# Strassen's products for both down-projections of a two-FFN decoder layer, with their activation sums made in the up-projection

## The chip, the cores and the metric

The kernel runs on one core of a Trainium2 chip. The time is device microseconds from start to end of one execution; three runs of the kernel before are shown, and one more execution was taken apart by the hardware profiler.

## What is computed

One layer of a hybrid decoder on 1024 prompt tokens and 32 sample tokens (1056 columns together): half a SwiGLU feed-forward block, token mixing (windowed attention beside a diagonal state-space scan), and a second half feed-forward block. All is float32. The change concerns the last product of the two feed-forward blocks, with D_MODEL = 1024 and D_FF = 2816:

```
def swiglu(x, w1, w3, w2):
    return (jax.nn.silu(x @ w1) * (x @ w3)) @ w2

def trunk_layer(x, pos0, k_buf, v_buf, s_re, s_im, p):
    x = x + 0.5 * swiglu(rms_norm(x, p['ffn1_norm']), p['ffn1_w1'], p['ffn1_w3'], p['ffn1_w2'])
    h = rms_norm(x, p['mix_norm'])
    ...
    x = x + merged @ p['w_out']
    x = x + 0.5 * swiglu(rms_norm(x, p['ffn2_norm']), p['ffn2_w1'], p['ffn2_w3'], p['ffn2_w2'])
```

## The kernel before

Activations lie with features on the 128 partitions and the 1056 tokens as columns. For precision each float32 operand is kept as two parts, a rounded high part (a cast on ScalarE) and the remainder (a subtraction on VectorE), and each product of 128x128 weights with a column group is three matmuls, high x high, high x remainder, remainder x high (`passes`, L225 to L229).

The program goes through these stages: first up-projection, first down-projection, the projections `pj` of the token mixing, scan and attention, w_out, second up-projection, second down-projection.

**Up-projection** (`up`, L385). D_FF is 22 blocks of 128 rows. Block by block, w1 and w3 are multiplied at once with Strassen's seven products over two halves of the model dimension and two halves of the tokens (H = 528 columns, each as two pieces J = 264). `wprep` makes the weight sums, `combos` made the sums of activations once for all blocks. Of the first two blocks the products are made in the plain way (`plain`). The results of product number 4, 3, 1, 2, 5, 7, 6, in this order, are put together by VectorE into a tile `e`, and the block is stored to `hid` in HBM, half by half (L411, L417). In the first up-projection a `hook` works in the parameters of the state-space scan (`params`, `params_b`) beside the blocks, on GpSimd, with some transposes on TensorE.

**Down-projection** (`down`, L421). Plain: the 22 blocks of `hid` are read back in groups of 4, 4, 4, 4, 4, 2 (`GROUPS`), each cut into high part `hh` and remainder `hl`; for each of the 8 output blocks and 3 column groups of 352 a PSUM bank collects a group's products, and VectorE adds half of it to the residual `x` (L445). In the first down-projection the last group's results also feed the next norm (`run_last`, `xg_part`): on ScalarE the scaled high part `xh` and a square, on VectorE the remainder `xl`, on GpSimd the sum of squares.

A scheduler sets the order of the instructions on each engine and of the loads in SP's single list, save where `in_order` (L139) pins TensorE, VectorE and ScalarE to the order of the code. Tiles come from pools: 34 large ones of 1056 columns (`T`), 4 for raw weights (`wr`, 4 KB a partition), 8 each for high parts and remainders of weights (`wh`, `wl`), 5 small ones (`sq`), and eight PSUM banks.

Lines of a helper stand for many calls: L229 is every such matmul, L81 every addition, subtraction or product of two tiles on VectorE or GpSimd, L93 every fused multiply-add on VectorE, L102 every activation, L208 and L334 casts of weights, L430 the cast of `hid`.

## Time and profile before

| | |
|---|---|
| median of three runs | 2161.9 us (2157.95 to 2163.28) |
| the profiled execution | 2159.04 us |
| its span in the trace | 2157.3 us |
| TensorE busy | 2095.9 us, 97% |
| VectorE busy | 1385.5 us, 64% |
| ScalarE busy | 749.2 us, 35% |
| GpSimd busy | 375.2 us, 17% |
| DMA | 234.4 MB, mean 109 GB/s |

In the profile PE is TensorE's matmuls, PEld its weight loads, DVE VectorE, ACT ScalarE, POOL GpSimd, SP the engine that issues the loads and stores. A group of instructions is named by the tile it writes and those it reads. An arrow (<-) behind idle time names what ended the wait.

### The profile page before, as it was taken

The page shows a single profiled execution, that of the slowest core. Times are in us where ns is not written, and L with a number is a line of the kernel's source. Part 1 is how long each engine was busy: PE and PEld are TensorE (multiplying, and loading weights), DVE is VectorE, ACT ScalarE, POOL GpSimd, SP SyncE. Part 2 cuts the span into 40 slices and gives each one's busy share as a digit, 9 for nine tenths or more (in the row PEclk, how much of TensorE's full clock was granted, in tenths as well). Part 3 has the DMA queues.
Part 4 walks back from the last instruction along what each step waited for, and adds up shares of the span by engine and source line. Part 5 has one row for each costly group of instructions (what it writes and reads, how often), then busy time and mean ns, then how long its engine had stood idle before and what let it go on. Part 6 is the DMA issues. An engine that isn't in the chain of part 4 may idle for free.

```text
span 2157.3 us, 38133 instructions
## 1 busy us (share of the span) xinstructions
PE 2095.9 (97%) x15058; PEld 2065.8 (96%) x15058; DVE 1385.5 (64%) x2485; ACT 749.2 (35%) x1464; POOL 375.2 (17%) x759
## 2 busy tenths in 40 slices
PE   8899999999999999999899899998999999999999
PEld 7899999988999999999899899988999999999999
DVE  5886666665554375757877857688666666565433
ACT  4432444344321152235555733343222232332110
POOL 0017777673000041324100200000000000000000
PEclk9899999999999999999999999999999999999999
DMA  4122322335631135632222373321222221363212
GB/s 164 36 88 73 115 95 86 122 103 169 227 117 55 60 120 184 213 108 62 80 88 82 144 247 125 124 88 45 78 90 67 82 89 62 100 238 124 81 35 81
DMA packets 133075, 234.40 MB, mean 109 GB/s; under 512 B 26064, under 2 KB 62736, under 8 KB 132880
## 3 DMA queue, kind: packets, MB, share of 16 engines
q1 hardware_dynamic: 132896, 231.97, 32.4%
q8 instruction: 118, 1.93, 0.4%
q14 instruction: 61, 0.50, 0.1%
HBM read 164.98 MB, written 64.06 MB: 106 GB/s over the span
## 4 chain that ended last, share of the span: by engine, by line
PE 87%; DVE 8%; ACT 2%; issue 2%; DMA 2%; SPq 0%; DVEq 0%; ACTq 0%
PE P L229 36%; PE p L229 26%; PE pj L229 13%; PE pm L229 4%; PE Q L229 2%; DVE wl L81 1%; PE pg L229 1%; PE ss L684 1%; DVE B L93 1%; DVE Xl L81 1%; PE po L1111 1%; PE sc L1072 1%; DVE e L81 1%; DVE B L81 0%; PE pt L1096 0%
## 5 line engine op out<-in xcount | busy, mean ns | idle before, releaser
L229 PE MATMUL P<-Xh,wh 128*128 128x264 f32 x2240 | 642.6, 287 | 21.4 <-DVE e L81 14.3
L229 PE MATMUL P<-Xl,wh 128*128 128x264 f32 x2240 | 641.0, 286 | 0.0
L229 PE MATMUL P<-Xh,wl 128*128 128x264 f32 x2240 | 639.4, 285 | 0.0
L229 PEld LDWEIGHTS P<-Xh,wh 128*128 128x128 f32 x2240 | 425.5, 190 | 26.6 <-DVE e L81 9.4
L229 PEld LDWEIGHTS P<-Xl,wh 128*128 128x128 f32 x2240 | 425.2, 190 | 1.5 <-issue 1.5
L229 PEld LDWEIGHTS P<-Xh,wl 128*128 128x128 f32 x2240 | 425.0, 190 | 0.0
L229 PE MATMUL p<-hh,wh 128*128 128x352 f32 x1056 | 341.6, 324 | 5.6 <-DVE x L93 2.8
L229 PE MATMUL p<-hh,wl 128*128 128x352 f32 x1056 | 341.5, 323 | 0.0
L229 PE MATMUL p<-hl,wh 128*128 128x352 f32 x1056 | 341.0, 323 | 0.0
L81 DVE TENSOR_TENSOR wl<-wr,wh 128x512 fp32r<-128x512 f32 (+1 forms) x360 | 249.4, 696 | 99.8 <-ACT wh L334 73.8
L93 DVE SCALAR_TENSOR_TENSOR x<-p,x 128x352 f32<-128x352 f32 x288 | 149.9, 523 | 238.2 <-PE p L229 235.7
L208 ACT CAST wh<-wr 128x512 fp32r<-128x512 f32 (+1 forms) x200 | 119.3, 601 | 429.9 <-PE p L229 309.0
L81 DVE TENSOR_TENSOR e<-e,P 128x528 f32<-128x528 f32 (+1 forms) x250 | 169.4, 680 | 136.3 <-PE P L229 116.8
L229 PE MATMUL pj<-xh,wh 128*128 128x352 f32 x624 | 205.2, 329 | 6.7 <-DVE gt L81 5.6
L229 PEld LDWEIGHTS p<-hh,wh 128*128 128x128 f32 x1056 | 198.5, 188 | 6.9 <-DVE x L93 3.4
L229 PE MATMUL pj<-xl,wh 128*128 128x352 f32 x624 | 203.6, 326 | 0.0
L229 PE MATMUL pj<-xh,wl 128*128 128x352 f32 x624 | 203.4, 326 | 0.0
L229 PEld LDWEIGHTS p<-hl,wh 128*128 128x128 f32 x1056 | 199.3, 189 | 0.0
L229 PEld LDWEIGHTS p<-hh,wl 128*128 128x128 f32 x1056 | 198.7, 188 | 0.0
L334 ACT CAST wh<-wr 128x512 fp32r<-128x512 f32 x160 | 98.9, 621 | 266.5 <-PE P L229 233.2
L334 ACT CAST wh<-ws 128x512 fp32r<-128x512 f32 x120 | 74.6, 622 | 228.3 <-PE P L229 220.5
L229 PEld LDWEIGHTS pj<-xh,wh 128*128 128x128 f32 x624 | 118.5, 190 | 8.2 <-DVE gt L81 6.1
(601 smaller groups left out, 3469.6 us busy)
## 6 DMA issues: line engine op xcount, KB each, us to landing
hr<-hid SPq DMA_DIRECT2D x44, 528.0 KB
hid<-e SPq DMA_DIRECT2D x78, 264.0 KB
wr<-in_w_in SPq DMA_DIRECT2D x26, 512.0 KB
wr<-in_w3a SPq DMA_DIRECT2D x40, 256.0 KB
wr<-in_w1a SPq DMA_DIRECT2D x40, 256.0 KB
wr<-in_w2a SPq DMA_DIRECT2D x40, 256.0 KB
wr<-in_w3b SPq DMA_DIRECT2D x40, 256.0 KB
wr<-in_w1b SPq DMA_DIRECT2D x40, 256.0 KB
```

The source lines that it names most:

```text
L81: e.tensor_tensor(out=o, in0=a, in1=b, op=op)
L93: V.scalar_tensor_tensor(out=o, in0=a, scalar=s, in1=b, op0=op0, op1=op1)
L208: S.copy(h[:, 0:m, :], r[:, i:i + m, :])
L229: mark["pe"] = PE.matmul(ps, a, b, start=first and i == 0, stop=last and i == 2, **kw).ins
L334: S.copy(h, s)
L684: PE.matmul(ps, f32(ones), s[:, kk, :], start=a + i + kk == 0, stop=a == 1 and i + kk == 2)
L1072: PE.matmul(o, st[e_][:, q0:q0 + 128], kk[:, k0:k0 + nk * 128], start=i == 0, stop=False)
L1111: PE.matmul(po[:, 0:256], Vs[blk // 4][:, blk % 4, m // 2, :], P[:, a_, kb * 256:kb * 256 + 256], start=i == 0, stop=i == 2 * nk - 1)
```

## The change

Both down-projections are made with Strassen's seven products too. Here the inner dimension is split by block number: blocks 2k and 2k+1 are a pair, 11 pairs (`NK`). The outputs split into two halves of 512 rows, the tokens into two halves of 528. One product at a time goes over four output blocks, each with a whole PSUM tile of two banks, and over the 11 pairs in three steps of 3, 4 and 4 pairs (`GROUPS`). `DOPS` gives the order of the products and the quarters of the result to which each is added with its sign; products 7 and 6 go on in the PSUM tiles of 4 and 3.

The seven combinations of activations are made in the up-projection: products 2 and 5 need a quarter as it is, the other five a sum or difference of two half blocks (`hsums`, on VectorE, through a small `sq` tile), and all are stored in seven arrays `hc` in place of `hid`. Only the two plain blocks still go through `hid` and are read back. `operands` reads one array two pairs at a time, casts and subtracts as before, reads one or two quarters of w2, adds them (`WCOMB`), casts and subtracts. While the matmuls of one step run, `down` draws the operands of the next, two pieces per output block, and the results of the output block before; the first step's operands are made in the last block of the up-projection. The next norm's parts (`xg_half`) follow in the middle step of the product after the one that finishes a quarter. The whole down-projection stands under `in_order`. The parameter work of the hook moves by one block, w2 is packed by quarters on the host.

```diff
-GROUPS = 4, 4, 4, 4, 4, 2
+NK = NFF // 2
+GROUPS = 3, 4, 4
+DOPS = (4, ((2, 1),)), (7, ((0, 1),)), (2, ((2, 1), (3, -1))), (1, ((0, 1), (3, 1))), (5, ((1, 1), (0, -1))), (3, ((1, 1),)), (6, ((3, 1),))
...
+        def hsums(k, e0, e1, do):
...
+            for op in do:
+                f_, a, b = {6: lambda: (add, half(e0, 0), half(e0, 1)), 4: lambda: (sub, half(e1, 0), half(e0, 0)),
+                            7: lambda: (add, half(e1, 0), half(e1, 1)), 3: lambda: (sub, half(e0, 1), half(e1, 1)),
+                            1: lambda: (add, half(e0, 0), half(e1, 1))}[op]()
+                t = SQ("hs", w=H)
+                f_(t, a, b)
+                mark["hid"] = dma(hc[op][:, k, :], t).ins
...
+                if f == NFF - 1:
+                    ks = first_operands(w2)
...
-                        dma(hid[f, :, 0:H].rearrange("p (j c) -> p j c", j=2)[:, js, :], q)
+                        if odd:
+                            hsums(k, e0, e, (4,))
+                        else:
+                            dma(hc[2][:, k, :].rearrange("p (j c) -> p j c", j=2)[:, js, :], q)
...
-                        mark["hid"] = dma(hid[f, :, H:T], e[:, H:T]).ins
+                        if odd:
+                            dma(hc[5][:, k, :], e[:, H:T])
+                            hsums(k, e0, e, (7, 3, 1))
+                        else:
+                            hsums(k, e, None, (6,))
+                if f == f0 + 1:
+                    es_ = [TT("e") for _ in range(2)]
+                    for i in range(2):
+                        dma(es_[i], hid[i])
...
+                    hsums(0, *es_, (6, 4, 7, 3, 1))
...
+        def operands(w, op, k0, n, ks):
+
+            for k1 in range(k0, k0 + n, 2):
+                m = min(2, k0 + n - k1)
...
+                dma(raw, hc[op][:, k1:k1 + m, :])
+                S.copy(h, raw)
+                p, q, f_ = WCOMB[op]
+                s = [wr_p.tile([128, 8, 128], F32, tag="wr", name="wr")[:, 0:4 * m, :] for i in (p, q) if i is not None]
+                for t, i in zip(s, (p, q)):
+                    dma(t.rearrange("p (k m) c -> p k (m c)", k=m), w[i % 2, i // 2, :, k1:k1 + m])
+                if q is not None:
+                    f_(s[0], s[0], s[1])
+                    yield
+                unit, low = w_cast(s[0], 4 * m)
+                sub(l, raw, f32(h))
+                yield
+                for a in low:
+                    sub(*a)
+                    yield
+                ks += [(unit[i], (h[:, i, :], l[:, i, :])) for i in range(m)]
...
+            for i, (op, outs, g) in enumerate(steps):
...
+                for m, p in enumerate(P):
+                    for k, (wu, (h, l)) in enumerate(ks, k0):
+                        for j in range(2):
+                            js = slice(j * J, j * J + J)
+                            passes(p[:, j, 0:J], [t[:, m, :] for t in wu], (h[:, js], l[:, js]), opens and k == 0, k == NK - 1,
+                                   skip_group_check=not opens)
+                    while evac:
+                        evac.pop(0)()
+                    for _ in range(2):
+                        next(it, None)
+                    if extra and g == 1:
+                        extra.pop(0)()
+                    if ends:
+                        evac.append(partial(evacuate, x, op, outs, m, p, done, extra, i + 1 == len(steps)))
...
+        WCOMB = {1: (0, 3, add), 5: (0, 1, add), 2: (2, 3, add), 7: (1, 3, sub), 6: (2, 0, sub), 3: (0, None, None), 4: (3, None, None)}
...
-                if f > 5 and f % 2:
+                if f > 4 and f % 2 == 0:
...
-        hid = dr.tile([NFF, 128, T], F32, name="hid")
+        hid = dr.tile([2, 128, T], F32, name="hid")
+        hc = {op: dr.tile([128, NK, H], F32, name=f"hc{op}") for op in OPS}
...
+        with in_order():
+            down(I["w2a"], I["x"], x, ks, (1, 2, 0, 3), xg_half)
...
+        with in_order():
+            down(I["w2b"], xd2, x, ks, (3, 1, 2, 0), lambda b, m: dma(O["y"][m, :, b * H:b * H + H], x[m][:, b * H:b * H + H]))
```

How this moves the instructions, at three places. Numbers behind a name tell one buffer's use from another's. First VectorE's list in the middle of the first down-projection: before, with the additions to `x` behind every output block and column group (`p2` is the PSUM tile).

```order
L81 TENSOR_TENSOR wl_7139<-wr_7136,wh_7138 128x512
L93 SCALAR_TENSOR_TENSOR x5_6693<-p2_6962,x5_6693 128x352
L81 TENSOR_TENSOR hl_7103<-hr_7100,hh_7102 128x1056
L93 SCALAR_TENSOR_TENSOR x5_6693<-p2_6976,x5_6693 128x352
L93 SCALAR_TENSOR_TENSOR x5_6693<-p2_6990,x5_6693 128x352
```

And now, in the middle step of product 1: the weight sum, the activation remainder, the norm's pieces, the weight remainders.

```order
L84 TENSOR_TENSOR wr_8124<-wr_8124,wr_8125 128x1024
L84 TENSOR_TENSOR hl_8121<-hr_8119,hh_8120 128x1056
L96 SCALAR_TENSOR_TENSOR xl_8137<-x4_6835,vec_84,xh_8136 128x528
L84 TENSOR_TENSOR wl_8130<-wr_8124,wh_8129 128x512
L84 TENSOR_TENSOR wl_8133<-wr_8124,wh_8132 128x512
L96 SCALAR_TENSOR_TENSOR xl_8169<-x5_6836,vec_84,xh_8168 128x528
L84 TENSOR_TENSOR sq_8172<-sq_8172,sq_8140 128x528
L84 TENSOR_TENSOR wr_8204<-wr_8204,wr_8205 128x1024
L84 TENSOR_TENSOR hl_8201<-hr_8199,hh_8200 128x1056
```

Before, a group's preparation lay between additions, and the sum of squares was GpSimd's; now the sums of weights and of squares have come to this list, and the additions stand at a product's end only.

Second SP's list in the same stretch, before: one quarter of a megabyte of weights at a time, activations up to two groups ahead.

```order
L198 DMA wr_7538<-in_w2a 128x512
L428 DMA hr_7514<-hid_133 128x1056
L428 DMA hr_7904<-hid_133 128x1056
L198 DMA wr_7544<-in_w2a 128x512
L428 DMA hr_7910<-hid_133 128x1056
L198 DMA wr_7550<-in_w2a 128x512
```

And now, around the loads of product 1:

```order
L430 DMA wr_8008<-in_w2a 128x1024
L425 DMA hr_7938<-hc1_136 128x528
L430 DMA wr_8009<-in_w2a 128x1024
L425 DMA hr_8003<-hc1_136 128x1056
L430 DMA wr_8063<-in_w2a 128x1024
L430 DMA wr_8064<-in_w2a 128x1024
L425 DMA hr_8058<-hc1_136 128x1056
L430 DMA wr_8124<-in_w2a 128x1024
```

Two loads of 1024 columns of weights now go with one of activations, and an activation load stands behind weight loads of the same or the next unit.

Third VectorE's list where a block of the first up-projection ends, before (`P3` is the last product's PSUM tile, the next `P1` the next block's second product):

```order
L81 TENSOR_TENSOR e_3218<-e_3218,P3_3377 128x528
L81 TENSOR_TENSOR wl_3773<-wr_3767,wh_3772 128x512
L81 TENSOR_TENSOR e_3218<-e_3218,a1_3219 128x528
L81 TENSOR_TENSOR wl_3777<-wr_3766,wh_3776 128x512
L81 TENSOR_TENSOR e_3447<-e_3447,P1_3475 128x528
```

And now, at the end of the second block of a pair:

```order
L84 TENSOR_TENSOR e_6073<-e_6073,P3_6234 128x528
L84 TENSOR_TENSOR wl_6564<-wr_6558,wh_6563 128x512
L84 TENSOR_TENSOR e_6073<-e_6073,a1_6074 128x528
L84 TENSOR_TENSOR hs_6262<-e_6073 128x528
L84 TENSOR_TENSOR hs_6265<-e_5710,e_6073 128x528
L84 TENSOR_TENSOR hs_6268<-e_5710,e_6073 128x528
L84 TENSOR_TENSOR wl_6568<-wr_6557,wh_6567 128x512
L84 TENSOR_TENSOR e_6313<-e_6313,P1_6341 128x528
```

Three sums have come in ahead of a weight remainder and of the next block's first addition. The remainders there belong to the block after the next one, in both.

## Rows read from the trace of the kernel before

**Rows 1.** Page, parts 1 and 4: busy time by engine; the chain that ended last

```profile
PE 2095.9 (97%) x15058; PEld 2065.8 (96%) x15058; DVE 1385.5 (64%) x2485; ACT 749.2 (35%) x1464; POOL 375.2 (17%) x759
...
PE 87%; DVE 8%; ACT 2%; issue 2%; DMA 2%; SPq 0%; DVEq 0%; ACTq 0%
PE P L229 36%; PE p L229 26%; PE pj L229 13%; PE pm L229 4%; PE Q L229 2%; DVE wl L81 1%; PE pg L229 1%; PE ss L684 1%; DVE B L93 1%; DVE Xl L81 1%; PE po L1111 1%; PE sc L1072 1%; DVE e L81 1%; DVE B L81 0%; PE pt L1096 0%
```

**Rows 2.** Chain in order of time: start us, us, what; the second feed-forward block

```profile
1507.74 381.26 PE P L229 x3143
...
1898.76 255.18 PE p L229 x1584
```

**Rows 3.** Windows: us, busy time of each engine, granted clock, DMA share, GB/s

```profile
98.00:530.00 432.00, 422.97 (x3416) 415.08 (x3416) 288.06 (x496) 168.09 (x339) 259.32 (x616) 0.99 0.31 102
531.00:765.00 234.00, 233.75 (x1448) 233.29 (x1449) 112.10 (x184) 47.90 (x68) 1.86 (x8) 1.00 0.36 119
1510.00:1890.00 380.00, 380.00 (x3137) 380.00 (x3136) 243.55 (x367) 113.49 (x188) 0.00 (x0) 1.00 0.24 81
1899.00:2154.00 255.00, 254.93 (x1584) 254.63 (x1583) 121.80 (x201) 41.66 (x56) 0.00 (x0) 1.00 0.33 108
```

**Rows 4.** Timeline of TensorE: starts of the two down-projections; idle time before, what ended it

```profile
531.25 0.43 PE L229 MATMUL p<-hh,wh 128*128 128x352 f32 x1 [1.88 <-DVE e L81]
...
1898.76 0.40 PE L229 MATMUL p<-hh,wh 128*128 128x352 f32 x1 [0.90 <-DVE e L81]
```

**Rows 5.** Chain in order of time, end of the first down-projection

```profile
791.40 7.01 PE pj L229 x42
```

**Rows 6.** Timeline of VectorE: the last result

```profile
2153.97 0.52 DVE L93 SCALAR_TENSOR_TENSOR x<-p,x 128x352 f32<-128x352 f32 x1 [0.44 <-PE p L229]
```

**Rows 7.** VectorE's groups by form, first down-projection: count, busy us, mean ns, idle before

```profile
L81 DVE TENSOR_TENSOR wl<-wr,wh 128x512 fp32r<-128x512 f32 x45 | 31.4, 697 | 0.0
L81 DVE TENSOR_TENSOR hl<-hr,hh 128x1056 fp32r<-128x1056 f32 x19 | 23.8, 1254 | 11.3 <-ACT hh L430 11.3
L93 DVE SCALAR_TENSOR_TENSOR xl<-x,vec,xh 128x352 fp32r<-128x352 f32 x24 | 17.7, 744 | 0.0
```

**Rows 8.** VectorE's groups by form, second up-projection

```profile
L81 DVE TENSOR_TENSOR e<-e,P 128x528 f32<-128x528 f32 x111 | 78.1, 703 | 69.1 <-PE P L229 67.0
...
L81 DVE TENSOR_TENSOR e<-e,a 128x528 f32<-128x528 f32 x19 | 13.3, 700 | 0.0
```

**Rows 9.** ScalarE's groups by form, first down-projection

```profile
L208 ACT CAST wh<-wr 128x512 fp32r<-128x512 f32 x45 | 27.8, 618 | 150.8 <-PE p L229 150.8
L430 ACT CAST hh<-hr 128x1056 fp32r<-128x1056 f32 x18 | 19.4, 1077 | 29.9 <-DMA hr<-hid 27.7 <-DVE wl L81 1.4 <-DVE hl L81 0.8
L102 ACT ACTIVATE xh<-x,vec 128x352 fp32r<-128x352 f32 x24 | 14.0, 587 | 7.5 <-DVE x L93 7.5
```

**Rows 10.** Windows while the second down-projection loads `x` (columns as in rows 3)

```profile
1902.00:1906.00 4.00, 4.00 (x27) 4.00 (x26) 1.90 (x4) 0.62 (x1) 0.00 (x0) 1.00 1.00 363
...
1910.00:1914.00 4.00, 4.00 (x27) 4.00 (x26) 1.74 (x3) 0.62 (x1) 0.00 (x0) 1.00 1.02 412
```

**Rows 11.** DMA around the start of the first down-projection, 500 to 560 us

```profile
DMA packets 5976, 14.56 MB, mean 243 GB/s; under 512 B 1181, under 2 KB 1437, under 8 KB 5955
...
q1 hardware_dynamic: 5971, 14.50, 69.5%
```

**Rows 12.** Timeline, second down-projection: one load's issue on SP, its first use on ScalarE

```profile
1930.99 0.38 SPq L428 DMA_DIRECT2D hr<-hid  x1
...
1934.72 1.08 ACT L430 CAST hh<-hr 128x1056 fp32r<-128x1056 f32 x1 [0.52 <-DMA hr<-hid]
```

**Rows 13.** TensorE's waits, 400 to 500 us: us in total, times, longest

```profile
PE P L229 <- DVE e L81: 4.5, 3, 2.1
```

**Rows 14.** SP's waits in the first up-projection: us in total, times, longest

```profile
SPq L586 <- POOL ta L81: 120.9, 8, 17.2
```

**Rows 15.** ScalarE's waits, 1890 to 1960 us: us in total, times, longest

```profile
ACT hh L430 <- DMA hr<-hid: 21.2, 12, 5.0
```

More of the change, by code (lines that the diff above doesn't have):

```diff
@@ L2 @@
 from contextlib import ExitStack, contextmanager
+from functools import partial
 from itertools import chain
@@ new lines, in first_operands, with down @@
+        def first_operands(w):
+            ks = []
+            rest(operands(w, DOPS[0][0], 0, GROUPS[0], ks))
+            return ks
+        def down(w, xd_, x, ks, order, done):
+            x.extend(TT(f"x{k}") for k in range(KD))
+            for k in range(KD):
+                dma(x[k], xd_[k])
+            steps = [(op, outs, g) for op, outs in DOPS for g in range(len(GROUPS))]
+            evac, extra = [], []
+            for i, (op, outs, g) in enumerate(steps):
+                n, k0 = GROUPS[g], sum(GROUPS[:g])
+                opens, ends = op not in (7, 6), k0 + n == NK
+                if opens and not g:
+                    P = [bank("pp", "D") for _ in range(4)]
+                    P = [P[t] for t in order]
+                nks, it = [], iter(())
+                if i + 1 < len(steps):
+                    it = operands(w, steps[i + 1][0], sum(GROUPS[:steps[i + 1][2]]), GROUPS[steps[i + 1][2]], nks)
+                for m, p in enumerate(P):
[12 more added lines that the diff above has]
+                        evac.append(partial(evacuate, x, op, outs, m, p, done, extra, i + 1 == len(steps)))
+                rest(it)
+                ks = nks
+            for f_ in evac + extra:
+                f_()
@@ new lines, in evacuate @@
+        def evacuate(x, op, outs, m, p, done, extra, last):
+            for c, sign in outs:
+                o = x[4 * (c // 2) + m][:, c % 2 * H:c % 2 * H + H].rearrange("p (j c) -> p j c", j=2)
+                stt(o, p[:, :, 0:J], 0.5 * sign, o, ALU.mult, ALU.add)
+            for c, _ in outs:
+                if op == LAST[c]:
+                    f_ = partial(done, c % 2, 4 * (c // 2) + m)
+                    if last:
+                        f_()
+                    else:
+                        extra.append(f_)
@@ L779, in body, with xg_half @@
             W0 = last_quarters(B, X, hid, ws, p11, raw2, cmb)
[L780 to L786 removed]
+        ks = up(*wa, I["w2a"], X, hid, 2, W0, hook)
+        banks(pp=(4, 2))
+        x = []
+        xsm, rm, accs, pend = {}, TT("rm"), {}, []
+        def xg_half(b, m):
+            if m not in xsm:
+                xsm[m] = XT("xh"), XT("xl")
+            hs = slice(b * H, b * H + H)
+            h, l = (t[:, hs] for t in xsm[m])
+            g, xc = vec[:, GM + m:GM + m + 1], x[m][:, hs]
+            act(h, xc, AF.Copy, scale=g)
+            stt(l, xc, g, f32(h), ALU.mult, ALU.subtract)
+            s = SQ("sq", w=H)
+            act(s, xc, AF.Square)
+            if b in accs:
+                add(s, s, accs[b])
+            accs[b] = s
+        with in_order():
+            down(I["w2a"], I["x"], x, ks, (1, 2, 0, 3), xg_half)
+        banks(mm=(4, 1), sm=(4, 1))
+        for b in range(2):
+            hl = [SQ("acc" + n, F32R, H) for n in "hl"]
+            S.copy(hl[0], accs[b])
+            sub(hl[1], accs[b], f32(hl[0]))
+            for j in range(2):
+                ps = SM("ss")[:, 0:J]
+                js = slice(j * J, j * J + J)
+                for i, a in enumerate(hl):
+                    PE.matmul(ps, ones, a[:, js], start=i == 0, stop=i == 1)
+                newton(rm[:, b * H + j * J:b * H + j * J + J], ps, SQ("y", w=J), SQ("a", w=J))
+        xsm = [xsm[m] for m in range(KD)]
         xd = dr.tile([KD, 128, T], F32, name="xd")
```

85 lines of the change are left out of this document (15 added, 70 removed).

## The prediction

> **What bounds the kernel now.** I read the page first, then the chain of waits in order of time, then windows over the four stages that the change touches, then the groups of instructions in those stages, and last the loads. TensorE is busy for 97% of the span and makes up 87% of the chain that ended last; the two groups of matmuls of the feed-forward blocks, `P` (up-projections) and `p` (down-projections and w_out), are 62% of it [rows 1]. So in these stages only work taken off TensorE, or a hole in it, changes the time. The chain shows the pieces to use: the second down-projection is one unbroken run of 1584 matmuls in 255.18 us, 161.1 ns each at 352 columns, and the second up-projection 3143 in 381.26 us, 121.3 ns each at 264 columns [rows 2]. Per column that is 0.458 and 0.459 ns: a narrower matmul costs nothing extra here. The windows show the same four stages by engine: TensorE full at a granted clock of 0.99 to 1.00, VectorE at 64 to 67% in the up-projections and at 48% in the down-projections, loads at 24 to 36% of the DMA engines [rows 3]. The room beside TensorE is what the change spends.
>
> The edges of the down-projections are nearly closed already. The first starts after a hole of 1.88 us, the second after 0.90 us [rows 4]. At the end of the first one VectorE works on the next norm, and the next stage (`pj`) starts at 791.40 [rows 5]. So the first down-projection, from the end of the up-projection at 529.4 to 791.4, takes 262.0 us; the second, from 1897.9 to its last result's start at 2153.97 [rows 6], takes 256.1 us.
>
> **TensorE's term.** Before: 22 row blocks x 8 output blocks x 3 column groups x 3 passes = 1584 matmuls of 352 columns. After: 7 products x 11 block pairs x 4 output blocks x 2 halves x 3 passes = 1848 of 264 columns. At 121.3 ns that is 224.2 us per down-projection, against 255.2 us of pure matmuls before: 31.0 us less, twice 62.0 us. The columns are exactly 7/8. This can't fail to happen, since the program's TensorE list grows by the 2 x 264 matmuls that this makes.
>
> **What must be hidden in exchange, VectorE first.** In a down-projection each step (one product, 3 or 4 of the 11 pairs) prepares the operands of the next, two pairs at a time; I call that a unit, 5.5 of them a product. Per unit VectorE does one weight sum of 1024 columns, one activation remainder of 1056 and two weight remainders of 512. The rows give 697 ns at 512 columns and 1254 ns at 1056 [rows 7], so 1.02 ns a column, and 1.22 us for the sum: 1.22 + 1.25 + 1.39 = 3.86 us. TensorE needs 48 x 121.3 ns = 5.82 us for a unit. A product with a weight sum costs VectorE 21.4 us (half a unit for the eleventh pair), and each of its results 4 additions of 528 columns, 0.70 us each by the nearest row, the PSUM addition of that width [rows 8]: 2.8 us, or 5.6 us where a product goes to two quarters. That is 24 to 27 us against TensorE's 264 x 121.3 ns = 32.0 us. In the second down-projection this fits everywhere.
>
> In the first one the next norm's work runs in the same list, four times for four blocks: a scaled remainder, 744 ns at 352 columns [rows 7], so 0.75 to 1.1 us at 528, and an addition of 0.70 us. The product after product 2 and the last product carry it beside their weight sums: 21.4 + 5.6 + 5.8 to 7.2 = 32.8 to 34.2 us against 32.0. So VectorE is the bound there by 1 to 2 us, and its steps are uneven: in the middle step it has 7.7 us of preparation plus about 6.4 us of norm, 14.1 us against TensorE's 96 x 121.3 ns = 11.6 us. The next step needs its first operands at its start and the second unit 12 matmuls (1.46 us) later, and the buffers for weight halves (8 of each kind, 3 or 4 in use per step) let the casts of a step begin only when the step before last has ended. Counting from that point: cast 0.62 us [rows 9], remainders 1.39, sum 1.22, remainder 1.25, remainders 1.39, about 6.1 us with 0.2 us of hand-over; plus three of the four norm pieces, 4.8 us: 10.9 us. The limit is 13.1 us. What can still make it late is a load. I put 3 us of holes on each of the two products. On the short steps (72 matmuls, 8.73 us) VectorE starts with 1.4 us of results of the product before, then 7.7 us: 9.1 us against 8.73 + 1.46; I put 1.5 us in all on these, in each down-projection. ScalarE needs 1.08 + 2 x 0.62 = 2.3 us for a unit, and for each norm piece two activations, 587 ns at 352 columns, so under 1.8 us together [rows 9]: never the bound.
>
> **The loads.** A unit with a weight sum now loads 2 x 512 KB of weights and 528 KB of activation sums: 1.59 MB in 5.82 us, 273 GB/s, where the stage now moves 108 to 119 GB/s [rows 3]. Is that to be had? While the second down-projection loads `x`, in rows of the same 4 KB, three windows of 4 us show from 363 to 412 GB/s, the first and the last of them standing here, at a DMA share of 1.00 to 1.02, and TensorE stays full [rows 10]. At the other end, the start of the first down-projection moved 243 GB/s over 60 us at 69.5% [rows 11], 350 GB/s if scaled to full. So 273 GB/s is 66 to 78% of what the engines give, and bandwidth is no bound. Latency: a single 528 KB load issued at 1930.99 is used by ScalarE at 1934.72, 3.7 us [rows 12]. Loads for a unit start when the buffers of the unit before last are free; from there it is the landing, then cast 1.08, remainders 1.25 and 1.39 us. This loop must close in two units' matmuls, 11.6 us, so it stalls only from a landing of 7.9 us on.
>
> One place is tighter. In the last product of the first down-projection, its two later steps load 8/11 of 8.74 MB, 6.4 MB, while four finished blocks of `x` go out, 2.2 MB: 8.5 MB in the 20.4 us of the steps before them, 417 GB/s. At the 412 GB/s of the best row that is 20.7 us, at 350 it is 24.3: 0 to 4 us of holes, and I take 2, the middle, since rows stand at both ends. The Trainium skill's page DMA: Bandwidth & Descriptors (Specifications) gives a core about 358 GB/s of HBM; by that figure the term would be 3.4 us and the sum 1.4 us larger, and the 412 GB/s row speaks against it as a ceiling for a core working alone.
>
> **The up-projections.** Each two row blocks get five sums of 528 columns on VectorE, 0.70 us each [rows 8], and their stores: 55 x 0.70 = 38.5 us per up-projection, from 243.6 to 282 of 380 us (74%) in the second [rows 3, 8]. They stand right behind the last result of a row block, ahead of one weight remainder; but the weights prepared there belong to a block two ahead, about 20 us away, so the cover is a whole block's matmuls. If it went, each set of three would cost 2.1 us. At the second block of each loop eight sums come close together over five buffers, so some wait for stores to land (3.7 us each by the nearest row): I put 1 us on each up-projection, bounds 0 and 4. The first up-projection has holes of 4.5 us where VectorE waited on late weights [rows 13], behind a store in SP's list that waited for GpSimd up to 17.2 us [rows 14]. The change moves that parameter work by one row block but leaves it in the same place relative to SP's list, so I leave those holes as they are (bounds: -4.5 and +5). The parameter work that now ends inside the first down-projection moves into the up-projection, on both sides under 1 us.
>
> **Edges and tail.** The first step's operands are made during the last row block; VectorE then has 3.5 us of the last block's sums and 5.3 us for the second step, 8.8 us, inside 8.73 + 1.46. I put 1 us on the first start and 0.5 on the second. At the end of the first down-projection the next stage's first 48 matmuls read columns finished two products earlier, so no hole there. The tail has one addition of 528 instead of 352 columns and a larger last store: +0.4 us.
>
> **The sum.** First down-projection 224.2 + 3 + 3 + 1.5 + 2 + 1 = 234.7; second 224.2 + 1.5 + 0.5 = 226.2; together 460.9 against 518.1: -57.2. Tail +0.4, up-projections +2: -54.8. The profiled execution's own time, 2159.0 us, becomes 2104.2; the median shown is 2.9 us (0.13%) above that execution, within the spread of the three, and I don't add it.
>
> **The rivals.** (1) *All of it hidden*: no holes in the down-projections, and the late weights of the first up-projection gone: 2159.0 - 518.1 + 448.4 + 0.4 = 2089.7, or 2085 with the second. For it: before, the same engines hid everything [rows 4]. Against: VectorE at 33 to 34 of 32 us. Chance 0.08. (2) *Steps start late*: every one of the 42 steps waits about half a microsecond for a last remainder or a load, because SP's single list makes a load wait behind another's buffer: +21, 2125. For it: at 108 GB/s ScalarE already waited 12 times for activations in 70 us, up to 5.0 us, without harm only because its lead is long [rows 15]; against: the limits worked out above leave 1 us or more. Chance 0.22. (3) *The sums hurt the up-projection*: buffers of the sums come free late behind SP's waits, and each two row blocks lose one set, 2.1 us x 20: 2146. The holes of 2.1 us seen now are of this kind [rows 13], but only in the first up-projection and only twice. Chance 0.05. (4) *The loads become the bound, slower than before*: two units take landing + 3.7 us; a down-projection has 7 x 5.5 = 38.5 units, so it is as slow as now when two take 258 / 38.5 x 2 = 13.4 us, a landing of 9.7 us. At 11 us: 14.7 / 2 x 38.5 = 283 us each, 2159 - 518 + 566 = 2207. Against it: 3.7 us for a lone load, and two more loads of its size ahead of it at 350 to 412 GB/s add under 3.2 us. Chance 0.04. The forecast gets the remaining 0.61.
>
> **How the numbers follow.** Predicted 2104. The forecast's own terms span about 2094 to 2113. Reaching from 2092 to 2128 takes in nearly all of that, most of rival 2 and part of rival 1: about 0.8. Only rival 4 is not faster by over 0.3% (6.5 us, about what a measurement of this kernel can tell from no change); between the signs hardly anything lies, so faster 0.95, same 0.01, slower 0.04.
>
> **What would show it.** Right: 1848 matmuls of 264 columns in each down-projection at 121 ns, TensorE full in the second one; VectorE near 100% in the two named products of the first, with holes of 1 to 3 us released by VectorE; DMA near 270 GB/s. Wrong: holes released by loads or ScalarE in most steps (rival 2 or 4), a pitch over 121.3 ns, or holes of about 2 us per two blocks in the up-projections (rival 3).

## The result: 1.5% faster, 33 us of the 55 forecast

The changed kernel takes 2128.55 us (median of 4 runs, 2126.27 to 2129.58) beside 2161.6 us (4 runs, 2157.95 to 2163.28) for the kernel before: 0.985 of its time, 95% interval 0.983 to 0.987. Forecast were 2104 us and a range of 2092 to 2128. The sign is right; the gain is 33 us instead of 55, and the time lies half a microsecond above the range. The profiled execution took 2128.92 us, its span is 2127.1.

The page of the changed kernel, parts 1 and 4, beside [rows 1]:

```profile
PE 2043.8 (96%) x15588; PEld 2012.1 (95%) x15588; DVE 1510.4 (71%) x2565; ACT 813.3 (38%) x1554; POOL 359.6 (17%) x735
...
PE 78%; DVE 8%; DMA 4%; POOL 4%; issue 3%; ACT 2%; SPq 1%; DVEq 0%; ACTq 0%; POOLq 0%
```

TensorE's busy time fell by 52 us, the span by 30. And GpSimd, which was in no share of the chain before, now makes 4% of it. The windows over the four stages, beside [rows 3], columns as there, each stage to its new end (the granted clock, third from the end, is the part of TensorE's full clock that it got):

```profile
98.00:556.00 458.00, 432.53 (x3420) 423.71 (x3420) 321.77 (x547) 168.43 (x342) 271.37 (x624) 0.97 0.38 125
557.00:788.00 231.00, 225.13 (x1848) 224.32 (x1848) 172.49 (x223) 102.42 (x152) 0.00 (x0) 1.00 0.78 268
1510.00:1897.00 387.00, 387.00 (x3191) 386.82 (x3189) 278.55 (x420) 114.40 (x190) 0.00 (x0) 1.00 0.35 122
1898.00:2123.00 225.00, 224.79 (x1848) 224.38 (x1848) 149.69 (x187) 78.66 (x111) 0.00 (x0) 1.00 0.73 250
```

Three of the four are as worked out: 1848 matmuls in about 225 us of TensorE, loads of 268 and 250 GB/s, the second up-projection full. The first up-projection is not: it ends 27 us later than before and had a mean granted clock of 0.97. The starts on TensorE's timeline and the last result on VectorE's, beside [rows 4 to 6], give the lengths:

```profile
557.27 0.36 PE L232 MATMUL D<-hh,wh 128*128 128x264 f32 x1 [0.89 <-DVE e L84]
...
789.07 0.63 PE L232 MATMUL pj<-xh,wh 128*128 128x352 f32 x1 [4.11 <-DVE x L96]
...
1897.92 0.36 PE L232 MATMUL D<-hh,wh 128*128 128x264 f32 x1 [0.89 <-ACT wh L211]
...
2123.04 0.71 DVE L96 SCALAR_TENSOR_TENSOR x<-D,x 128x528 f32<-128x528 f32 x1 [2.19 <-PE D L232]
```

| piece | before | forecast | after |
|---|---|---|---|
| end of the first up-projection | 529.4 | +1 | 556.4 (+27.0) |
| first down-projection | 262.0 | 234.7 | 232.7 |
| from there to the end of the second up-projection | 1106.5 | +1 | 1108.0 (+1.5) |
| second down-projection to its last result | 256.1 | 226.2 | 226.0 |
| from the last result to the end | 3.3 | +0.4 | 4.1 (+0.7) |

So the expected gain was made, and almost half of it was lost again in the stage ahead of it. TensorE's waits between 95 and 560 us (total, times, longest), the kernel before first:

```profile
PE P L229 <- DVE e L81: 10.0, 7, 3.6
PE p L229 <- DVE e L81: 1.9, 1, 1.9
PE P L229 <- ACT e L396: 1.8, 2, 0.9
```

and the changed one:

```profile
PE P L232 <- DVE e L84: 17.7, 9, 3.6
PE pk L660 <- ACT c L648: 8.4, 1, 8.4
PE P L232 <- ACT e L380: 2.9, 3, 1.1
```

The 1.9 us for `p` before lie behind the end of the stage; two waits under 1 us aren't shown. Within the up-projection TensorE waited 12.2 us before and 29.0 us now: 16.8 us more. The rest is clock. Four windows of the changed kernel (the granted clock is the number before the DMA share):

```profile
200.00:250.00 50.00, 41.57 (x318) 40.45 (x317) 29.34 (x45) 16.32 (x35) 37.94 (x98) 0.90 0.32 108
...
210.00:215.00 5.00, 0.53 (x3) 0.41 (x4) 0.00 (x0) 1.42 (x4) 4.61 (x12) 0.52 0.57 180
215.00:220.00 5.00, 5.00 (x24) 4.59 (x22) 3.15 (x6) 3.13 (x8) 4.46 (x10) 0.50 0.53 197
...
400.00:450.00 50.00, 47.37 (x372) 46.20 (x371) 34.67 (x51) 18.55 (x38) 35.70 (x79) 0.97 0.34 108
```

Before, the granted clock was 1.00 from 150 us to the end of the stage. Now the stop of 8.4 us ends at 214.5, and of the two levels, 2.4 and 1.2 GHz, the clock is at the lower one from about 210 to 221 us. In the first four of these us TensorE stood still, which costs nothing; in the other six it worked at half its pace, 3.0 us lost. From 350 us to the end of the stage, with stops of 2 to 4 us in it, the mean is 0.97 over 206 us: 6.2 us more, nearly all of it with TensorE working. With the waits that makes 26.0 of the 27.0.

**What stands behind it.** GpSimd works through eight parameter blocks beside the row blocks, one per two of them. SP's single list has, per parameter block, the store `pb_d<-ta` of GpSimd's result, at which SP waits until GpSimd is done, and behind it the loads of w3 and w1, the stores of the sums, and the load `in_bc` with which GpSimd begins the next block. SP's timeline, then GpSimd's first operation, of the changed kernel:

```profile
420.60 0.33 SPq L634 DMA_DIRECT2D pb_d<-ta  x1
421.02 0.38 SPq L676 DMA_DIRECT2D pb_d<-tp  x1
421.50 0.89 SPq L286 DMA_DIRECT2D wr<-in_w3a  x2
422.48 0.88 SPq L286 DMA_DIRECT2D wr<-in_w1a  x2
423.45 0.38 SPq L357 DMA_DIRECT2D hc<-hs  x1
423.92 0.38 SPq L405 DMA_DIRECT2D hc<-e  x1
424.36 0.48 SPq L608 DMA_DIRECT2D tb<-in_bc  x1
...
467.95 0.32 SPq L634 DMA_DIRECT2D pb_d<-ta  x1
```

```profile
431.04 0.60 POOL L84 TENSOR_TENSOR tb<-tb,par 128x32 f32<-128x32 f32 x2 [10.43 <-DMA tb<-in_bc]
```

From one store to the next 47.35 us: 10.4 until GpSimd begins, 36.9 of its own work. TensorE needs 42.7 us for two row blocks with the transposes between them (the pace of the runs below in which nothing holds it). So the loop of GpSimd and SP was the slower one, and the w1 loads came when it let them. They hold VectorE's list, in which the results `e` stand that TensorE waits for; VectorE's longest waits from 330 to 505 us are for them:

```profile
DVE ws L84 <- DMA wr<-in_w1a: 22.8, 4, 7.4
```

Was it new? My theory A: GpSimd's loop sets the pace, and VectorE's sums make GpSimd slower. The rivals: B, VectorE's own load makes the weights late; C, the parameter work coming one row block earlier; later D, buffers that are held longer.

### The profile page after: what moved, and what is told of

It is laid out like the page before. It is cut to its first block, busy times and chain, and to the rows that moved or that the text cites. A ratio compares the mean times of both kernels' runs of the same rounds, so it can differ in the third digit from the quotient of the medians.

```text
span 2127.1 us, 39676 instructions
## 1 busy us (share of the span) xinstructions
PE 2043.8 (96%) x15588; PEld 2012.1 (95%) x15588; DVE 1510.4 (71%) x2565; ACT 813.3 (38%) x1554; POOL 359.6 (17%) x735
## 4 chain that ended last, share of the span: by engine, by line
PE 78%; DVE 8%; DMA 4%; POOL 4%; issue 3%; ACT 2%; SPq 1%; DVEq 0%; ACTq 0%; POOLq 0%
PE P L232 32%; PE D L232 18%; PE pj L232 13%; PE pm L232 4%; PE p L232 3%; POOL tb L84 3%; PE Q L232 2%; DMA hr<-hc 2%; DVE wl L84 2%; PE pg L232 1%; POOL ta L84 1%; DMA wr<-in_w1a 1%; DVE e L84 1%; PE ss L733 1%; DVE B L96 1%
## 5 line engine op out<-in xcount | busy, mean ns | idle before, releaser
L232 PE MATMUL D<-hh,wl 128*128 128x264 f32 x1232 | 349.3, 284 | 2.7 <-DVE wl L84 2.7
L232 PE MATMUL D<-hh,wh 128*128 128x264 f32 x1232 | 349.7, 284 | 1.8 <-DVE e L84 0.9
L232 PE MATMUL D<-hl,wh 128*128 128x264 f32 x1232 | 350.1, 284 | 0.1
L84 DVE TENSOR_TENSOR wl<-wr,wh 128x512 fp32r<-128x512 f32 (+1 forms) x426 | 289.8, 696 | 64.2 <-ACT wh L301 44.3
L232 PEld LDWEIGHTS D<-hh,wl 128*128 128x128 f32 x1232 | 231.5, 188 | 3.3 <-DVE wl L84 3.3
L232 PEld LDWEIGHTS D<-hh,wh 128*128 128x128 f32 x1232 | 232.0, 188 | 2.1 <-issue 1.1
L211 ACT CAST wh<-wr 128x512 fp32r<-128x512 f32 (+1 forms) x266 | 153.3, 605 | 209.8 <-DVE wr L84 66.6
L232 PEld LDWEIGHTS D<-hl,wh 128*128 128x128 f32 x1232 | 231.6, 188 | 0.3 <-DVE hl L84 0.3
L232 PE MATMUL pj<-xh,wh 128*128 128x352 f32 x624 | 205.3, 329 | 10.4 <-DVE gt L84 5.2
L426 ACT CAST hh<-hr 128x1056 fp32r<-128x1056 f32 x84 | 84.2, 1003 | 191.5 <-DMA hr<-hc 188.9
L84 DVE TENSOR_TENSOR hl<-hr,hh 128x1056 fp32r<-128x1056 f32 x84 | 97.8, 1164 | 79.7 <-ACT hh L426 79.4
```

What stands on the lines that cost most here:

```text
L84: e.tensor_tensor(out=o, in0=a, in1=b, op=op)
L211: S.copy(h[:, 0:m, :], r[:, i:i + m, :])
L232: mark["pe"] = PE.matmul(ps, a, b, start=first and i == 0, stop=last and i == 2, **kw).ins
L426: S.copy(h, raw)
```

## The experiments

Each kernel ran beside runs of the kernel before on its own chip, whose medians are 2159.9 to 2163.0 us.

| kernel | median us | ratio to before (95%) |
|---|---|---|
| changed | 2128.55 | 0.983 to 0.987 |
| e1_bc_ahead | 2122.88 | 0.980 to 0.984 |
| e2_no_sums | 2123.99 | 0.981 to 0.984 |
| e3_old_blocks | 2134.82 | 0.986 to 0.989 |
| e4_bc_ahead_old_blocks | 2107.17 | 0.973 to 0.976 |
| b2_dummy_sums (on the kernel before) | 2187.51 | 1.011 to 1.014 |
| b3_dummy_psum (on the kernel before) | 2173.61 | 1.004 to 1.007 |
| b1_bc_ahead (on the kernel before) | 2151.36 | 0.994 to 0.997 |
| e5_bc_spare | 2109.81 | 0.974 to 0.978 |
| e6_store_late | 2107.44 | 0.974 to 0.977 |
| e10_late_sums4 | 2099.46 | 0.969 to 0.974 |
| e12_late_old_last | 2094.05 | 0.967 to 0.971 |
| e13_bc_old_last | 2107.41 | 0.973 to 0.977 |

From the timelines, as means over the parameter blocks (seven from store to store, five for the changed kernel from 279.73 on), in us:

| kernel | store to store | until GpSimd begins | its own stretch |
|---|---|---|---|
| before | 44.1 | 9.2 | 34.9 |
| before with dummy sums (b2) | 47.5 | 9.4 | 38.1 |
| before with dummy additions from PSUM (b3) | 44.5 | 9.3 | 35.2 |
| changed | 46.9 | 9.8 | 37.1 |
| changed without sums (e2) | 45.4 | 10.6 | 34.8 |

**e1_bc_ahead.** The load taken out of the loop, by one more large buffer.

```diff
@@ load_consts
+            bcs.append(TT("bcs")[:, 0:NB * 128].rearrange("p (b c) -> p b c", b=NB))
+            dma(bcs[0].rearrange("p b (q i c) -> p b q i c", q=4, i=2), I["bc"].rearrange("b p q i c -> p b q i c"))
@@ params_b
-            bc = tb[:, 0:128].rearrange("p (q i c) -> p q i c", q=4, i=2)
+            bc = bcs[0][:, b].rearrange("p (q i c) -> p q i c", q=4, i=2)
-            dma(bc, I["bc"][b])
```

> The changed kernel, with the eight parameter blocks' inputs bc loaded once, ahead, into one buffer of their own, so that GpSimd waits for no load at the start of a block (10.2 to 10.4 us of idle per cycle in the changed kernel). Theory A (GpSimd's parameter loop, its own work plus the wait for this load behind SP's single list, sets the pace of the first up-projection): the stores pb_d<-ta come every 41 to 43 us instead of every 46 to 48, no more VectorE wait for the w1a load after the third parameter block, end of the first up-projection from 556.4 to 535 - 540 us, total 2128.6 - 15 to -20 = 2108 - 2114. Theory B (VectorE's own load, the five sums, makes the weights late): under 3 us, 2126 - 2129. Theory C (only the parameter work being one row block earlier): under 3 us as well.

Measured: 2122.88 us, 5.7 us less. The first blocks ran at 43 us, then the pace fell back to 45.5 to 47. GpSimd's waits from 330 to 505 us:

```profile
POOL ta L630 <- issue: 16.4, 2, 8.2
POOL ta L630 <- DMA hc<-e: 9.8, 1, 9.8
```

No load any more, but a wait as long before the first write of `ta`, which takes one of the 34 large buffers. Once the profile names what ended it, the store of a block `e` (the other two times it shows nothing); that store stands in SP's list behind `pb_d<-ta`. In the changed kernel a pair's first block stays until the sums are made, and this edit took one buffer more: theory D. A wait had taken the place of the one removed, and theory A's number fell short.

**e2_no_sums.** Part of the computation is left out: in the first up-projection the first operand is stored in place of the sum.

```diff
-        def hsums(k, e0, e1, do):
+        def hsums(k, e0, e1, do, raw=False):
...
+                if raw:
+                    mark["hid"] = dma(hc[op][:, k, :], a).ins
+                    continue
                 t = SQ("hs", w=H)
                 f_(t, a, b)
...
-                            hsums(k, e, None, (6,))
+                            hsums(k, e, None, (6,), hook)
```

> The changed kernel without the five sums per two row blocks in the first up-projection: the first operand is stored unsummed with the same stores, so VectorE does 55 additions of 528 columns less there (about 38 us of work), and what the first down-projection then computes is not the reference. Theory A: GpSimd's busy time per parameter block falls from 33.3 - 34.1 to about 31.6 us, the cycle from 46 - 48 to 43 - 45.7 us, and 8 x 2 us = 13 to 17 us come back: 2111 - 2116. Theory B: all 27 us come back: 2101. Theory C: under 3 us, 2126 - 2129.

Measured: 2123.99, only 4.6 us less. GpSimd's stretch went back to 34.8 us as A has it, but it began 0.8 us later than in the changed kernel, and the loop is still 2.7 us longer than TensorE's. The up-projection ended 10.3 us earlier; in the first down-projection ScalarE waited for a load of `hr`, TensorE 3.8 us for ScalarE, and the granted clock was 0.91 from 560 to 600 us, which gave 7.5 us back. B is out as the whole cause: without a single sum 17 of the 27 us are still there, and the second up-projection, with the same sums on VectorE and nothing on GpSimd, has TensorE full. A got its mechanism, not its 13 us.

**e3_old_blocks.** The hook on odd row blocks again.

```diff
- if f > 4 and f % 2 == 0:
+ if f > 5 and f % 2:
- elif f > 3 and f % 2 == 0 and f < 4 + 2 * NB:   # params_b((f - 4) // 2)
+ elif f > 4 and f % 2 and f < 5 + 2 * NB:        # params_b((f - 5) // 2)
```

> The changed kernel with the parameter work hooked to the same row blocks as in the kernel before (odd ones, one later). Theory C: all 27 us come back, 2101. Theory A: the hole of 8.4 us at the first pk and the clock of 0.90 after it come back (about 10 us), the 46 to 48 us cycle stays: 2117 - 2124. Theory B: the same hole at most: 2117 - 2129.

Measured: 2134.82, 6.3 us more; every theory expected less. The early hole is gone, but the loop is unchanged at 47.3 us, its last store came at 535.88 instead of 513.99, and a hole of 10.5 us follows at the end. Where a loop sets the end, a later start is a later end. C is out as the whole cause; what the earlier row block costs by itself shows only where the loop no longer holds the stage (e12 beside e6, below).

**e4_bc_ahead_old_blocks.** Both edits.

> Both edits at once: bc loaded ahead, and the parameter work on the row blocks of the kernel before. Theory A: the early hole and the pace are both gone, the first up-projection ends at 525 - 532 us, total 2098 - 2106, faster than either edit alone. Theory B: 2117 - 2129. Theory C: 2101, no faster than the later row blocks alone.

Measured: 2107.17, 21 us less, though the one alone gave 6 and the other cost 6. The stores come every 42.7 us, TensorE is full from 200 to 500 us at a clock of 1.00, and the up-projection still ends only at 533.5, after a single hole at its end:

```profile
PE pk L663 <- ACT c L651: 10.4, 1, 10.4
```

**b2_dummy_sums, b3_dummy_psum.** To see what the sums alone do, the kernel before got five more additions per two row blocks at the same places, without stores: in b2 with both operands in `e`, in b3 with a half of `e` and a product in PSUM.

```diff
# b2
+                        if hook and f % 2:
+                            add(SQ("hs", w=H), e[:, 0:H], e[:, 0:H])
...
+                        for _ in range((3 if f % 2 else 1) if hook else 0):
+                            add(SQ("hs", w=H), e[:, 0:H], e[:, H:T])
# b3, at the same two places
+                            add(SQ("hs", w=H).rearrange("p (j c) -> p j c", j=2), q, p)
...
+                            add(SQ("hs", w=H).rearrange("p (j c) -> p j c", j=2), g, p)
```

> The kernel before, with five more VectorE additions of 528 columns per two row blocks in the first up-projection, at the places where the changed kernel has its sums; their results go nowhere, no store and no buffer of a block is held longer. The down-projections are the old ones. Theory A (VectorE's extra work slows GpSimd's parameter block, which with its idle time of 10 us per block is already as long as two row blocks of TensorE): GpSimd busy per block from 31.7 to 33 - 34 us, pb_d<-ta every 46 to 48 us instead of 43 to 45.7, end of the first up-projection 15 to 25 us later, 2162 + 15 to 25 = 2177 - 2187. Rival D (the pace was lost to buffers, since the changed kernel holds each block's result e until the sums of the pair are made): the additions cost under 4 us, 2160 - 2166.

> The kernel before with the same five extra VectorE additions of 528 columns as in b2_dummy_sums, at the same places, but each adds a half block e to a product still in PSUM instead of adding two halves of SBUF; results go nowhere. VectorE is given the same number of additions. In b2_dummy_sums GpSimd's operations took 0.79 to 0.91 us while sums of two SBUF operands ran and 0.44 to 0.48 us beside an addition that read PSUM. Theory A1 (the sums cost by slowing GpSimd, each by what both read from SBUF): GpSimd's stretch from its start to the store stays at 35 to 36 us per block instead of 37.3 to 39.0, and of the 26 us of b2_dummy_sums under 9 are left: 2162 - 2170. The Trainium skill's page SBUF — State Buffer (section SBUF: two separate sides) has such a rule, by which it would be the same. Theory A2 (VectorE's own time: it is late for the weights, whatever it reads): 2180 - 2187, as in b2_dummy_sums.

Measured: b2 2187.51, 26 us more than before; GpSimd's stretch rose from 34.9 to 38.1 us and the loop to 47.5. That is as much as the changed kernel lost in this stage, made by 50 additions, 35 us at 0.70, that VectorE had room for. b3: 2173.61, 10.6 us more, a little above the expected 9; the stretch stays at 35.2 and the loop at 44.5. So of the 26 us some 15 hang on where the second operand is read. Of its own it has waits of 6.8 us for `pk` and 3.5 us at the start of the down-projection. Whether those come from the products being held longer in PSUM wasn't tried. VectorE's timeline of b2, then GpSimd's:

```profile
367.93 0.70 DVE L81 TENSOR_TENSOR e<-e,P 128x528 f32<-128x528 f32 x1 [2.66 <-PE P L229]
368.55 1.01 DVE L81 TENSOR_TENSOR hs<-e 128x528 f32<-128x528 f32 x1
...
371.20 2.74 DVE L81 TENSOR_TENSOR hs<-e 128x528 f32<-128x528 f32 x3
```

```profile
367.96 0.49 POOL L81 TENSOR_TENSOR tb<-tb,pwr 128x128 f32<-128x128 f32 x1
...
371.71 0.79 POOL L81 TENSOR_TENSOR tb<-tb,pwn 128x144 f32<-128x144 f32 x1
372.47 0.91 POOL L81 TENSOR_TENSOR tb<-tb,pwr 128x144 f32<-128x144 f32 x1
373.45 0.84 POOL L81 TENSOR_TENSOR tb<-tb 128x144 f32<-128x144 f32 x1
```

Beside the addition that reads PSUM GpSimd's operation takes 0.49 us; beside the three sums one takes 0.79 to 0.91, and each sum 0.91. In b3, VectorE's three dummies and GpSimd beside them:

```profile
358.02 1.91 DVE L81 TENSOR_TENSOR hs<-e,P 128x528 f32<-128x528 f32 x3
```

```profile
358.36 0.44 POOL L81 TENSOR_TENSOR tb<-tb,pwr 128x144 f32<-128x144 f32 x1
358.88 0.50 POOL L81 TENSOR_TENSOR tb<-tb 128x144 f32<-128x144 f32 x1
359.45 0.44 POOL L81 TENSOR_TENSOR tb<-tb,pwr 128x144 f32<-128x144 f32 x1
```

0.64 us a dummy, and GpSimd undisturbed. In the changed kernel the same shows in the sums themselves, first in the first up-projection (200 to 510 us), then in the second, where GpSimd does nothing (count, busy us, mean ns):

```profile
L84 DVE TENSOR_TENSOR hs<-e 128x528 f32<-128x528 f32 x32 | 25.7, 833 | 0.4
...
L84 DVE TENSOR_TENSOR hs<-e 128x528 f32<-128x528 f32 x52 | 35.0, 705 | 2.0 <-DMA hc<-hs 1.0
```

The two engines take turns when each reads two operands from SBUF. The Trainium skill's page SBUF — State Buffer (SBUF: two separate sides) says so: an operation of VectorE with two inputs in SBUF and one of GpSimd that reads SBUF exclude each other for the length of a whole instruction. These rows agree.

**b1_bc_ahead.** The edit of e1 on the kernel before.

> The kernel before, with bc loaded once, ahead, into one buffer of the T pool, as in the first experiment of this kind. If the idle time of 10 us of GpSimd per block is what puts the kernel before at the edge (theory A), the ten microseconds of TensorE's waits for late weights there go, and the parameter blocks come at TensorE's own 42.5 us: 2150 - 2155. If another wait takes the load's place, as in the changed kernel with the same edit: 2157 - 2163.

Measured: 2151.36, 10.2 us less. TensorE is full from 200 to 500 us and the stores come every 42.6 us from the second one on. Of the 10.0 us that TensorE waited for `e` before, 4 lie ahead of 120 us and stay; the other 6 are gone, and the stage ends 7.4 us earlier. So in the kernel before GpSimd's loop was already the bound of this stage, by 1.4 us a block. The one buffer less does no harm here, where no first block of a pair is held: GpSimd begins within 1 us of the store.

**e5_bc_spare.** The load one parameter block ahead, into columns of `vec` that hold the scan's start state. The scan reads those columns later and here finds other values: this kernel leaves the start state out.

```diff
+        def bc_at(b):
+            o = S0 + 128 * (b % 2)
+            return vec[:, o:o + 128].rearrange("p (q i c) -> p q i c", q=4, i=2)
@@ params_b
-            dma(bc, I["bc"][b])
+            if not b:
+                dma(bc, I["bc"][b])
+            elif b + 1 < NB:
+                dma(bc_at(b + 1), I["bc"][b + 1])
...
             yield
+            if not b:
+                dma(bc_at(1), I["bc"][1])
```

> The changed kernel with bc loaded one parameter block ahead as in e1_bc_ahead, but into columns that lie idle in another constant, so that the T pool keeps its 34 buffers (e1_bc_ahead took one). Rival D (GpSimd's start then waits for a buffer of the T pool, which a stored block e frees): with the buffer given back GpSimd starts within 3 us, the pace stays at TensorE's 42.5 us, only the early hole of about 9 us with its lower clock is left: 2106 - 2112. If the wait for the store of e stays as in e1_bc_ahead, so that one buffer is not the point: 2119 - 2126.

Measured: 2109.81, as D expected. Against e1 the T pool has its buffer back, and that is 13 us; GpSimd still waits for `ta` six times, up to 7.9 us. So the load taken out of the loop is enough to bring the blocks to 42.7 to 45.1 us, if no buffer is taken for it: load and buffer are two ways in which GpSimd's start hangs on SP's list.

**e6_store_late.** Only the store is put behind the transposes' stores in SP's list.

```diff
- dma(pb_d[b, :, 512:1024], ta[:, 512:1024])
...
- dma(pa_d[b, :, i * 256:i * 256 + 256], mt.rearrange("p a m -> p (a m)"))
+ st = dma(pa_d[b, :, i * 256:i * 256 + 256], mt.rearrange("p a m -> p (a m)")).ins
+ with tc.issue_after(st):
+     dma(pb_d[b, :, 512:1024], ta[:, 512:1024])
```

> The changed kernel with the store pb_d<-ta, at which SP's list waits for GpSimd, put behind the stores of the transposed half (some 13 us later in SP's list); nothing else moved. Theory A: the w1a loads and the load of bc no longer stand behind that wait, so bc has landed and its buffer alone can hold GpSimd; TensorE's waits for e after 300 us (about 15 us) go, the early hole of 8.4 us stays: 2106 - 2114. If the weights were late for another reason (VectorE's list): 2125 - 2129.

Measured: 2107.44, 21 us less, from the place of one store. The stores come every 42.7 us with all sums made. TensorE's waits, 95 to 560 us:

```profile
PE P L232 <- DVE e L84: 6.8, 2, 6.4
PE P L232 <- ACT e L380: 2.9, 3, 1.1
```

**e10_late_sums4, e12_late_old_last, e13_bc_old_last.** What is left: the early hole (e6), the late one (e4).

```diff
# e10: e6 and
- if f == f0 + 1:          # sums of the first two blocks
+ if f == f0 + 2:
# e12: e6, the hook of e3, and after product 4 of the last block
# e13: e4, and the same
+ if hook and f == NFF - 1:
+     hook(f, False)
```

> e6_store_late, with the five sums of the first pair of row blocks made one row block later, so that VectorE's list has them behind the start of the parameter work. In e6_store_late one early hole of 6.4 us with a granted clock of 0.93 is left between 200 and 250 us, and no other loss before the down-projection. If it is there because VectorE gives GpSimd its first operands 15 us later than in the kernel before, it shrinks under 3 us and the clock returns to 1.00: 2107.4 - 5 to -9 = 2098 - 2102. If it comes from the parameter work being one row block earlier alone: 2106 - 2109.

> The changed kernel with the late store of e6_store_late and the parameter work on the row blocks of the kernel before, whose last second half is started after the first product of the last row block instead of after the sixth, ahead of the down-projection's first operands on ScalarE. Theory A: pace of TensorE (42.7 us per parameter block), no early hole, the 10.4 us hole of e4_bc_ahead_old_blocks at the end gone: 2094 - 2100. If the two kinds of work still collide in the last row block: 2103 - 2110.

> e4_bc_ahead_old_blocks (bc loaded ahead, parameter work on the row blocks of the kernel before), its last second half started after the first product of the last row block. The 10.4 us hole there and the granted clock of 0.89 to 0.92 after it should go: 2107.2 - 8 to -12 = 2095 - 2099; if the collision stays: 2104 - 2110.

Measured: e10 2099.46, within what was expected, with a hole of 3.0 us left; GpSimd got its first operands of the parameter work at 151.22 instead of 158.09 (e6), before the change at 143.93. e13 2107.41, no gain over e4: a miss. In the last block ScalarE waited 9.7 us to copy, for the buffers that the store `pa_d<-mt` frees, and that store stands behind `pb_d<-ta` and two loads of `x` in SP's list. ScalarE's timeline:

```profile
519.39 0.87 ACT L653 COPY c<-tb 64x288 f32<-64x288 f32 x2 [9.68 <-DMA pa_d<-mt]
```

It looks like the same head of the queue again (no run takes only that away), and e12, which has the late store, doesn't have it: 2094.05 us, 0.969 of the kernel before, the fastest of all. Its windows of the first two stages and TensorE's waits, 95 to 560 us:

```profile
98.00:522.00 424.00, 422.09 (x3420) 415.22 (x3420) 319.09 (x547) 167.18 (x342) 279.39 (x616) 0.99 0.41 138
523.00:754.00 231.00, 226.70 (x1848) 225.76 (x1847) 172.90 (x222) 102.59 (x153) 3.03 (x8) 0.99 0.77 265
```

```profile
PE P L232 <- DVE e L84: 4.1, 2, 3.6
PE P L232 <- ACT e L380: 1.8, 2, 0.9
```

Its first up-projection ends at 521.9, 7.5 us earlier than in the kernel before, with 31 us more of VectorE's work in it: the change's whole gain, and what the old loop cost.

## Why the prediction was right and wrong

**Right: TensorE's term and the two down-projections.** 1848 matmuls at 121.3 ns were to be 224.2 us; with their waits forecast 234.7 and 226.2, measured 232.7 and 226.0. The loads came at 268 GB/s in the first, forecast 273, and no wait of TensorE between its steps was longer than 2.3 us: rivals 2 and 4 didn't come.

**Right in sum, wrong in its parts: the holes of the first down-projection.** I put 3 us on each of two products where VectorE was to be the bound. VectorE was busy at most 42.5 of 50 us there (650 to 700), and TensorE's waits for remainders are 2.5 us, 2.3 of them in the last product. Ahead of that one ScalarE had waited 4.3 us for a load of `hr`, so it may be the load that I had priced at 2 us as well as VectorE; no run tells them apart. The first edge of 1 us was 0.89. On the other hand I saw no hole at the next stage's start; there TensorE waited 4.1 us for the last result, 1.7 to 4.1 us with the variants.

**Wrong: one step, the first up-projection.** The prediction says of the parameter work that the change "leaves it in the same place relative to SP's list, so I leave those holes as they are", with bounds of -4.5 and +5. The stage became 27 us longer. The place did stay the same. What I didn't do is to add up GpSimd's loop as I added up TensorE's and VectorE's: 34.9 us of work and 9.2 us until it begins are 44.1, against 42.7 for TensorE. [Rows 14] said that SP waited for GpSimd in each of the eight blocks, 120.9 us in all, up to 17.2 at a time, and [rows 13] that TensorE waited behind it. An engine with a busy share of 17% over the span [rows 1] was at its limit in this stage: 259 of 432 us [rows 3], and the rest not free either, but waiting for SP.

So the 38.5 us of sums were priced on the wrong engine. VectorE did have the room (it is at 70% in the stage), and in b3 the same number of additions costs 10.6 us in place of 26. Most of their cost is what they take from GpSimd: five sums a parameter block, each lengthening GpSimd's stretch by up to its own 0.7 us, are up to 3.5 us; b2 measured 3.2, the changed kernel 2.2. In a loop without slack that comes back at every one of the eight blocks: in b2 the first store is 5.0 us later than before and the last 28.9.

The ends of the stage say what part of the 27 us the loop made. Where nothing holds TensorE it ends at 521.9 (e12). The kernel before, at 529.4, was 7.5 us behind that by its loop. The changed kernel, at 556.4, is 34.5 behind: 24.7 go with the late store alone (e6, 531.7), the other 9.8 are the early hole, which e12 has not, with the parameter work one row block later again and its last half started earlier. How much of this the sums make depends on where one starts: put into the kernel before they cost 26 us (b2), taken out of the changed one they give back 10.3 (e2), where the loop is too slow without them as well.

By the rule of the Trainium skill's page SBUF — State Buffer (SBUF: two separate sides), with five sums of 0.70 us a block [rows 8], an estimate for the stage would have been 7 x 3.5 = 25 us in place of my 1, and 2128 in all. That it meets the measured time so well is luck: it has neither the early hole nor the slower loop of e2 in it.

**Rival 3** named the right stage and the right work, at 2146 with a chance of 0.05, but another mechanism (small buffers, in both up-projections). The second one, which has the same sums and no GpSimd work, lost 1.5 us in all. **Rival 1**, which had the late weights of the first up-projection go away as well, is what e12 shows to be within reach, at 2094 against its 2085.

What stays open: why the pace without sums (e2) is still 45.4 us, 1.3 more than before. One store more stands between SP's store and the load there, 4.3 to 5.7 us from one to the other, before 3.7 to 4.3: 0.8 us on the mean. The rest comes behind the load's issue. No run takes only one of these away. Open too is the cause of b3's 10.6 us.

## What to carry to other kernels

Add up every loop that crosses a queue, engine by engine, with the waits between its parts, in the stage itself: an engine at 17% of the span can be the pace of one stage. Price an operation added to VectorE also on GpSimd, where both read two operands from SBUF. And where a store waits in the single list of loads for a slow engine, what stands behind it waits too: moving that one store further down the list gave 21 us, beside 33 for the whole change.

## What was not expected of the hardware

VectorE and GpSimd alternate instruction by instruction when both read two operands from SBUF: a GpSimd product of 128x144 takes 0.44 to 0.50 us beside additions that read PSUM and 0.79 to 0.91 beside a sum of 528 columns from SBUF, which itself takes 0.91 in place of the 0.64 of an addition that reads PSUM. And holes cost more than their length, but less than the mean clock makes one think: around an 8.4 us stop of TensorE the granted clock is 0.90 over 50 us, 10 us at the lower level, but four of them lie in the stop, and only the six behind it cost, 3.0 us; with the holes gone (e12) the clock is 1.00 from 150 to 500 us.
